# A diffusion backbone on one core: the first layer's FFNs in pairs by seven block products, and its row products moved

## The chip, the core and the metric

The kernel runs on one core of a Trainium2 chip. TensorE (PE) does the matmuls; VectorE (DVE), ScalarE (ACT) and GpSimd (POOL) do the elementwise work; SyncE (SP) issues the loads. The metric is the device time of one execution. The kernel before takes 2105.61 us, the median of three runs between 2104.49 and 2106.18 us.

## The reference

Two layers work on 256 latent and 256 context tokens of width 1024. Cut to what matters here:

```python
for l in range(DEPTH):
    mod = (silu_c @ w_ada[l] + b_ada[l])          # 9 x 1024 values: shift, scale, gate
    mod_c = (silu_cc @ w_ada[l] + b_ada[l])       # the same for the context
    x  = x  + 0.5 * g1  * swiglu(modulate(rmsnorm(x),  sh1,  sc1),  w1, w3, w2)   # d_ff 2816
    xc = xc + 0.5 * cg1 * swiglu(modulate(rmsnorm(xc), csh1, csc1), w1, w3, w2)
    o_lat, o_ctx = token_mixer(...)               # retention + latent attention, gated merge
    x  = x + g2 * o_lat
    x  = x + 0.5 * g3 * swiglu(...)               # the second FFN
    if not last:
        xc = xc + cg2 * o_ctx
        xc = xc + 0.5 * cg3 * swiglu(...)
return rmsnorm(x, final_norm)

def swiglu(h, w1, w3, w2):
    return (silu(h @ w1) * (h @ w3)) @ w2
```

The last layer's second FFN works on the latent tokens alone.

## The kernel before

Activations are kept transposed: eight tiles of 128 channels by 512 tokens, the latent ones in columns 0 to 255, the context's in 256 to 511. Every fp32 matmul is made of three single-pass ones: each operand is split into a high half (`hi`, rounded) and a low half (`lo` = operand - `hi`), and W.hi X.hi + W.lo X.hi + W.hi X.lo is accumulated (`mm3`). A weight tile is one chunk of 512 KB: SP loads it into one of four `raw` buffers, ACT writes its high half (`wh<-raw`), DVE its low half (`wl<-raw,wh`; four buffers of each). A chunk of kind `"d"` has the low half made without DVE: ACT writes the negative and a DMA from POOL's queue adds the operand (`wl<-raw`, `wl<-t`).

An FFN has 22 tiles of the inner width, worked off in parts. Each part does its up tiles (`up`: 24 matmuls of 512 columns for a tile of w1, 24 for a tile of w3, then silu, product and split into `G`), and then eight down tiles over the part's inner tiles (`down`), each of which updates x. `PARTS` are (0,6), (6,14), (14,22). In the first FFN's first part two more up tiles are computed early (`N_EARLY`). The last three down tiles of an FFN are worked in two halves of 256 columns (`tail`).

The first FFN of the second layer, (1, 2) in `PAIRED`, has the parts (0,4), (4,10), (10,16), (16,22). In its first part it works as above. After that it takes two inner tiles at a time: the weight tiles m and m+1 and the tokens (latent, context) form a 2x2 block product, which is done by seven half-size products in place of eight, by Winograd's form of Strassen's scheme. `blocks` builds the combined token operands t1 to t4 once, at the end of the first part. `split_pair` builds the combined weights of each pair: POOL makes s1 and s3, DVE s2 and s4, and each is then split into halves. `pair` issues the products: 84 matmuls of 256 columns, with four adds on DVE to combine them; two of its products are left for the next step (`pend`, `flush`).

The modulation values are dot products of rows of `w_ada` with silu(c). For all but the first two and the last of the 18 they are made by DVE: `ada_steps` loads eight chunks of 512 KB per value into `raw` buffers, and DVE multiplies each with the row of silu(c) and sums (`junk<-raw,crow`), in the first layer a second time for the context's row. They are called row products here. `ada_fill(n)` adds credit after a step and puts as many queued chunks there as the credit allows; `ada_flush` puts in all that must be done by then. `FILL` holds the credits.

All steps of the program go through `Plan`. It keeps an ordered list of all operations with a priority each (the place in the list; `ahead` moves one forward, row products are moved 200 back), gives each an assumed cost, and replays them engine by engine: whichever engine is free takes the waiting operation of the best priority whose inputs are ready and whose buffers (51 tiles `t`, 14 `u`, four `raw`, ...) can be had. This fixes each engine's order of instructions, which the hardware then keeps. `run_steps` issues loads and splits four chunks ahead of the step that uses them.

In the profile nearly all instructions carry line 378 of the kernel before, the line in `Plan.emit` that issues them (382 after the change); they are told apart by the names of their tiles.

Of the kernel before, what the change touches and what calls it, by code (L numbers as in the profile page):

```python
# [18 lines left out]
P = 128  # L19
KD = 8  # L20
# [431 lines left out]
def kernel(  # L452
# [152 lines left out]

    def split_pair(r0, r1):
# [14 lines left out]
        W["s4"] = halves(s4, hi[:, TOK:], lo[:, TOK:], S_DMA)  # L621
        W["a22"] = halves(a22, T(dt=F32R), T(dt=F32R))
        return W

    def run_steps():
        flat = [c for ch, _ in steps for c in ch]
        raws, ready = [], []

        def dma_to(n):
            for ap, size, _ in flat[len(raws):n]:  # L630
                raws.append(plan.new("raw", size))
                sp.dma_start(out=raws[-1], in_=ap)

        def split_to(n):
            dma_to(n)
            for i in range(len(ready), min(n, len(flat))):
                kind = flat[i][2]
                ready.append(split_pair(raws[i - 1], raws[i]) if kind == "p" else split_w(raws[i], flat[i][1], kind))
# [276 lines left out]
    def ffn(l, w1, w3, w2, m_sh, m_g, nrm_in, nrm_out, n_tok, n_next, fill, pre=None):  # L915
# [162 lines left out]
        for pi, (k0, k1) in enumerate(parts):  # L1078
# [4 lines left out]
            for m in range(at, until):  # L1083
                if pre and m < NS:
                    continue
                if paired and pi:
                    if (m - k0) % 2 == 0:
                        for j, w in enumerate((w1, w3)):
                            step(pair(j, m), chunk(w[l, m]), chunk(w[l, m + 1], kind="p"))
                elif m >= N_FIRST or pre:  # L1090
                    step(up(m), chunk(w1[l, m]), chunk(w3[l, m]))
# [13 lines left out]
            for m in range(KD - n_tail):  # L1105
                nrm = nrm_out if last else None
                step(down(m, k0, k1, nrm, 0, n_tok, m == KD - 1), chunk(w2[l, m, :, k0 * P:k1 * P], n))
                if m % 2 == 0 and not last:
                    ada_fill(FILL[0])
            if n_tail:  # L1110
# [16 lines left out]
    def mixer(l, nrm_in, nrm_out, full):  # L1127
# [461 lines left out]

        proj = [(rqk(RQ, i, NQ, 1.0), W("q", i)) for i in range(N_RQ[l], 4)]  # L1590
        proj += [(rqk(RK, i, TOK, RET_SCALE), W("k", i)) for i in range(4)]
        proj += [(rv(n, c), chunk(w_v[l, n, c])) for n in range(2) for c in range(4)]
        att = []
# [12 lines left out]
        for i, (f, w) in enumerate(proj):  # L1606
# [304 lines left out]
```

## Time and profile before

| what | value |
| --- | --- |
| median of three runs | 2105.61 us |
| the profiled execution | 2105.88 us |
| its span | 2104.1 us |
| PE busy | 2084.1 us (99%) |
| DVE busy | 1499.7 us (71%) |
| ACT busy | 839.4 us (40%) |
| POOL busy | 254.5 us (12%) |
| granted PE clock, mean | 0.996 |

The span runs from the first to the last instruction; the time of the execution is somewhat longer. An engine is busy while an instruction of it is under way; PE and the weight loads (PEld) overlap, and so do the ends of instructions that follow each other. A stretch of the span can be asked for by itself: the busy time of each engine in it, and the number of its instructions. The stretches below begin at the first matmul of a weight tile. In FFN1 of the first layer inner tiles 3 to 7 begin at 63.69 us, the first down tiles at 119.49, inner tiles 8 to 13 at 152.86. Merge (the gates, the MLA and retention outputs) is taken from the first MLA output tile at 681.81; its retention output tiles are 782.11 to 826.36. In FFN2 of the first layer the first down tiles begin at 940.24 and inner tiles 6 to 13 at 973.68. The second layer's paired FFN begins at 1241.86 us, its pairs at 1310.35, and its tail at 1579.37.

### The profile page before, as it was taken

What the parts mean: (1) busy time and instruction counts of PE and PEld (TensorE: products, weight loads), DVE (VectorE), ACT (ScalarE), POOL (GpSimd) and SP (SyncE); (2) the same over time, 40 slices, a digit from 0 to 9 for tenths busy, and PEclk for the clock granted to TensorE, in tenths of its full rate; (3) what the DMA queues carried; (4) which work ended last, traced back from release to release, by engine and by line L of the source; (5) the groups of instructions that cost most, each with busy time, mean ns of one, the idle gap of its engine ahead of it and who ended that gap; (6) DMA issues with size and microseconds to landing.
All of it is one profiled execution on the core that took longest, in us unless ns stands there. A gap on an engine that the chain in (4) does not pass through costs nothing.

```text
span 2104.1 us, 31948 instructions
## 1 busy us (share of the span) xinstructions
PE 2084.1 (99%) x12328; PEld 1816.7 (86%) x12328; DVE 1499.7 (71%) x2797; ACT 839.4 (40%) x1445; POOL 254.5 (12%) x268
## 2 busy tenths in 40 slices
PE   9999999999999999999999999999999999999998
PEld 7888888987788888988888898989999879999998
DVE  6898875678678435888865478877867867666655
ACT  5222122566443222422222243645456646344443
POOL 0000000211142000100000021332422114000000
PEclk9999999999999999999999999999999999999999
DMA  8476554221252333366655433654543326574653
GB/s 321 160 221 206 187 187 130 88 91 55 65 137 81 112 119 104 130 204 214 202 189 191 129 101 100 150 146 117 158 114 111 103 68 163 169 263 149 202 183 108
DMA packets 95722, 311.73 MB, mean 148 GB/s; under 512 B 10577, under 2 KB 13777, under 8 KB 95569
## 3 DMA queue, kind: packets, MB, share of 16 engines
q1 hardware_dynamic: 88082, 291.87, 42.9%
q0 software_dynamic: 7488, 17.83, 4.7%
q8 instruction: 97, 1.59, 0.3%
q14 instruction: 55, 0.45, 0.1%
HBM read 290.78 MB, written 1.05 MB: 139 GB/s over the span
## 4 chain that ended last, share of the span: by engine, by line
PE 90%; DVE 5%; DMA 2%; issue 1%; ACT 1%; POOL 1%; SPq 0%; POOLq 0%; DVEq 0%; ACTq 0%
PE m L378 82%; PE a L378 8%; DVE t L378 2%; DVE u L378 1%; DVE wl L378 1%; DMA wl<-t 1%; ACT wh L378 0%; DVE s L378 0%; DMA raw<-in_w3a_dram 0%; ACT t L378 0%; POOL t L378 0%; DMA x<-in_xT_dram 0%; POOL s L378 0%; DMA raw<-in_w1b_dram 0%; SPq L378 0%
## 5 line engine op out<-in xcount | busy, mean ns | idle before, releaser
L378 PE MATMUL m<-t,wh 128*128 128x512 f32 (+1 forms) x6236 | 1570.1, 340 | 2.4 <-DVE t L378 1.7
L378 PEld LDWEIGHTS m<-t,wh 128*128 128x128 f32 x6236 | 1073.6, 188 | 143.6 <-issue 1.9
L378 PE MATMUL m<-t,wl 128*128 128x512 f32 (+1 forms) x3118 | 1051.9, 339 | 0.6 <-DMA wl<-t 0.5
L378 ACT CAST wh<-raw 128x1024 fp32r<-128x1024 f32 (+2 forms) x388 | 391.8, 1011 | 753.7 <-PE m L378 609.0
L378 PEld LDWEIGHTS m<-t,wl 128*128 128x128 f32 x3118 | 587.0, 188 | 70.4 <-DMA wl<-t 1.2
L378 DVE TENSOR_TENSOR wl<-raw,wh 128x1024 fp32r<-128x1024 f32 (+2 forms) x372 | 437.3, 1177 | 177.3 <-ACT wh L378 175.4
L378 DVE SCALAR_TENSOR_TENSOR junk<-raw,crow 128x1024 f32<-128x1024 f32 x220 | 269.1, 1223 | 51.1 <-DMA raw<-in_w_ada_dram 48.5
L378 DVE SCALAR_TENSOR_TENSOR x<-m,mod,x 128x256 f32<-128x256 f32 x208 | 93.4, 479 | 102.4 <-PE m L378 101.9
L378 ACT ACTIVATE t<-m 128x512 f32<-128x512 f32 (+1 forms) x137 | 68.7, 503 | 243.3 <-PE m L378 240.0
L378 POOL TENSOR_TENSOR s<-s,mhalf 128x2 f32<-128x2 f32 (+1 forms) x31 | 32.5, 1053 | 1075.5 <-DVE s L378 1075.4
L378 DVE TENSOR_TENSOR t<-t,t 128x512 fp32r<-128x512 f32 (+7 forms) x234 | 137.7, 597 | 6.7 <-ACT t L378 4.0
L378 PE MATMUL m<-t,t 128*128 128x256 f32 (+1 forms) x696 | 102.3, 299 | 0.0
L378 PEld LDWEIGHTS m<-t,t 128*128 128x128 f32 x696 | 91.1, 190 | 4.0 <-issue 0.8
L378 PE MATMUL m<-wh,t 128*128 128x512 f32 x288 | 92.0, 399 | 0.0
L378 PE MATMUL a<-t,t 128*64 128x256 f32 (+3 forms) x512 | 87.6, 350 | 3.9 <-DVE t L378 3.8
L378 DVE TENSOR_TENSOR t<-t,m 128x512 f32<-128x512 f32 (+1 forms) x73 | 42.0, 577 | 64.3 <-PE m L378 63.2
L378 PEld LDWEIGHTS a<-t,t 128*128 128x128 f32 (+1 forms) x512 | 65.5, 175 | 20.2 <-DVE t L378 3.4
L378 DVE TENSOR_TENSOR u<-u,u 128x256 f32<-128x256 f32 x127 | 54.5, 447 | 14.4 <-ACT u L378 13.9
L378 PEld LDWEIGHTS m<-wh,t 128*128 128x128 f32 x288 | 53.1, 188 | 12.4 <-issue 1.2
L378 ACT CAST t<-t 128x512 fp32r<-128x512 f32 (+4 forms) x112 | 56.0, 527 | 12.2 <-DVE t L378 9.8
L378 PE MATMUL a<-t,wh 128*128 128x256 f32 x288 | 56.9, 281 | 0.0
L378 PE MATMUL m<-wl,t 128*128 128x512 f32 x144 | 56.7, 394 | 0.0
(127 smaller groups left out, 1574.8 us busy)
## 6 DMA issues: line engine op xcount, KB each, us to landing
raw<-in_w_ada_dram SPq DMA_DIRECT2D x122, 512.0 KB, 4.2
raw<-in_w_m_dram SPq DMA_DIRECT2D x76, 512.0 KB, 3.7
raw<-in_w1b_dram SPq DMA_DIRECT2D x44, 512.0 KB, 3.7
raw<-in_w3b_dram SPq DMA_DIRECT2D x44, 512.0 KB, 4.1
raw<-in_w1a_dram SPq DMA_DIRECT2D x41, 512.0 KB, 3.7
raw<-in_w3a_dram SPq DMA_DIRECT2D x41, 512.0 KB, 3.8
raw<-in_w2b_dram SPq DMA_DIRECT2D x32, 512.0 KB, 3.5
raw<-in_w2a_dram SPq DMA_DIRECT2D x32, 384.0 KB, 3.2
```

Source lines behind the costliest of these rows:

```text
L378: call(*[resolve(v) for v in args], **{k: resolve(v) for k, v in kwargs.items()})
```

## The change

FFN1 (0, 2) and FFN2 (0, 8) of the first layer get entries in `PAIRED`: FFN1 with the parts (0,6), (6,12), (12,18), (18,22), FFN2 with the parts of the second layer's. All parts but the first of each are worked in pairs. `S_DMA` becomes a table of which low halves of a pair are made by DMA: s4 alone, where s3 and s4 were; this holds for the second layer too. `FILL` becomes a table by layer and place. `BY_DMA` names the mixer's weights whose low half is made by DMA: `g` as before, and now each third of the first layer's `gr` and of the second layer's `gm`, and each second of the first layer's `v`.

```diff
-PAIRED = {(1, 2): ((0, 4), (4, 10), (10, 16), (16, 22))}
+PAIRED = {(1, 2): ((0, 4), (4, 10), (10, 16), (16, 22)), (0, 8): ((0, 4), (4, 10), (10, 16), (16, 22)),
+          (0, 2): ((0, 6), (6, 12), (12, 18), (18, 22))}
-S_DMA = True
+S_DMA = {2: ("s4",), 8: ("s4",)}
-FILL = (2,0,0,.5)
+FILL = {(0, 2): (.5, 1.5), (0, 8): (.5, 1), (1, 2): (.25, 1), (1, 8): (2, 2), 0: (.5, 0, 3), 1: (0, .75, .25)}
+BY_DMA = {("g", 0): 1, ("g", 1): 1, ("gr", 0): 3, ("gm", 1): 3, ("v", 0): 2}
...
-        W["s3"] = halves(s3, hi[:, 0:TOK], lo[:, 0:TOK], S_DMA)
+        W["s3"] = halves(s3, hi[:, 0:TOK], lo[:, 0:TOK], "s3" in by_dma)
...
+    def way(name, phase, i):
+        n = BY_DMA.get((name, phase), 0)
+        return "d" if n and i % n == 0 else "w"
...
-                            step(pair(j, m), chunk(w[l, m]), chunk(w[l, m + 1], kind="p"))
+                            step(pair(j, m), chunk(w[l, m], kind="d" if "a1" in S_DMA[m_g] else "w"), chunk(w[l, m + 1], kind=S_DMA[m_g]))
...
-                ada_fill(EARLY_FILL if pre and pi == 0 else FILL[0])
+                ada_fill(EARLY_FILL if pre and pi == 0 else FILL[l, m_g][0])
...
                 if m % 2 == 0 and not last:
-                    ada_fill(FILL[0])
+                    ada_fill(FILL[l, m_g][1])
...
-            ada_fill(FILL[1])
+            ada_fill(FILL[l][0])
...
-            step(g_step(i), W("g", i, "d"))
+            step(g_step(i), W("g", i, way("g", l, i)))
...
-            ada_fill(FILL[3])
+            ada_fill(FILL[l][2])
```

PE, first layer, FFN1: the first matmuls of inner tile 8. `wh`, `wl` are the halves of the tile of w1, the moving `t` are halves of the normalised tokens, `m` and `a` are PSUM tiles. Before:

```order
L378 MATMUL m2_1425<-t26_317,wh2_1336 128x512
L378 MATMUL m2_1425<-t26_317,wl2_1343 128x512
L378 MATMUL m2_1425<-t29_327,wh2_1336 128x512
L378 MATMUL m2_1425<-t39_375,wh2_1336 128x512
L378 MATMUL m2_1425<-t39_375,wl2_1343 128x512
L378 MATMUL m2_1425<-t42_386,wh2_1336 128x512
```

After, at the same place, rows eight to twelve of the first product and the start of the next:

```order
L382 MATMUL a0_1526<-t4_441,wl2_1433 128x256
L382 MATMUL a0_1526<-t2_458,wh2_1421 128x256
L382 MATMUL a0_1526<-t9_501,wh2_1421 128x256
L382 MATMUL a0_1526<-t9_501,wl2_1433 128x256
L382 MATMUL a0_1526<-t12_517,wh2_1421 128x256
L382 MATMUL m2_1547<-t0_857,wh3_1462 128x256
L382 MATMUL m2_1547<-t0_857,wl3_1479 128x256
L382 MATMUL m2_1547<-t49_867,wh3_1462 128x256
L382 MATMUL m2_1547<-t0_857,wh3_1462 128x256
L382 MATMUL m2_1547<-t0_857,wl3_1479 128x256
```

The wide accumulation over 512 tokens gives way to products of 256 columns; the one into `m2` has combined tokens (`t0`, `t49`) and combined weights (`wh3`).

SP, first layer, merge: loads between two MLA output tiles (`w_mo`); `w_m` are gate weights, `w_ada` row-product chunks, and the number after `raw` is the buffer. Before:

```order
L378 DMA raw0_6157<-in_w_mo_dram 128x1024
L378 DMA raw3_6206<-in_w_ada_dram 128x1024
L378 DMA raw3_6311<-in_w_m_dram 128x1024
L378 DMA raw2_6334<-in_w_m_dram 128x1024
L378 DMA raw1_6365<-in_w_mo_dram 128x1024
L378 DMA raw0_6408<-in_w_m_dram 128x1024
L378 DMA raw3_6451<-in_w_m_dram 128x1024
L378 DMA raw2_6487<-in_w_mo_dram 128x1024
L378 DMA raw1_6522<-in_w_ada_dram 128x1024
L378 DMA raw0_6552<-in_w_m_dram 128x1024
```

After:

```order
L382 DMA raw0_7040<-in_w_ada_dram 128x1024
L382 DMA raw2_7093<-in_w_ada_dram 128x1024
L382 DMA raw3_7242<-in_w_ada_dram 128x1024
L382 DMA raw1_7291<-in_w_m_dram 128x1024
L382 DMA raw1_7413<-in_w_m_dram 128x1024
L382 DMA raw0_7424<-in_w_mo_dram 128x1024
L382 DMA raw2_7460<-in_w_ada_dram 128x1024
L382 DMA raw1_7466<-in_w_ada_dram 128x1024
L382 DMA raw0_7507<-in_w_ada_dram 128x1024
L382 DMA raw3_7527<-in_w_m_dram 128x1024
```

Three chunks of row products stand in a row where one stood now and then, in three of the four buffers.

POOL, second layer, the first pair steps of the paired FFN: two adds that make s1 and s3, and the DMAs of low halves. Before:

```order
L378 TENSOR_TENSOR t42_11257<-raw3_11224 128x512
L378 TENSOR_TENSOR t46_11270<-raw2_11213,raw3_11224 128x512
L378 TENSOR_TENSOR t18_11312<-raw1_11277 128x512
L378 TENSOR_TENSOR t32_11329<-raw0_11245,raw1_11277 128x512
L378 DMA wl1_11338<-t46_11270 128x512
L378 DMA wl1_11338<-t44_11304 128x512
```

After:

```order
L382 TENSOR_TENSOR t49_13805<-raw2_13767 128x512
L382 TENSOR_TENSOR t17_13818<-raw0_13755,raw2_13767 128x512
L382 TENSOR_TENSOR t7_13838<-raw1_13798 128x512
L382 TENSOR_TENSOR t48_13855<-raw3_13779,raw1_13798 128x512
L382 DMA wl1_13887<-t27_13876 128x512
```

The DMA into the low half of s3 (the one from `t46`, written by the add before) is gone; that half is now a subtract in DVE's order.

## Rows read from the trace of the kernel before

**Rows 1.** The page: busy time of each engine, and the chain that ended last.
```profile
PE 2084.1 (99%) x12328; PEld 1816.7 (86%) x12328; DVE 1499.7 (71%) x2797; ACT 839.4 (40%) x1445; POOL 254.5 (12%) x268
...
PE 90%; DVE 5%; DMA 2%; issue 1%; ACT 1%; POOL 1%; SPq 0%; POOLq 0%; DVEq 0%; ACTq 0%
```

**Rows 2.** Busy times by stretch, first layer: two FFNs, then merge. Columns in the first line.
```profile
core 0: us, PE busy (x) PEld busy (x) DVE busy (x) ACT busy (x) POOL busy (x), PEclk, DMA share, GB/s
63.69:119.49 55.80, 55.80 (x241) 45.05 (x240) 48.33 (x81) 11.39 (x15) 0.00 (x0) 1.00 0.59 187
119.49:152.86 33.37, 33.37 (x146) 27.04 (x145) 31.27 (x54) 7.35 (x8) 0.00 (x0) 1.00 0.70 225
152.86:219.80 66.94, 66.94 (x289) 54.06 (x288) 56.19 (x93) 15.53 (x18) 0.00 (x0) 1.00 0.65 206
940.24:973.68 33.44, 33.44 (x145) 27.05 (x144) 30.85 (x55) 7.35 (x8) 0.00 (x0) 1.00 0.65 206
973.68:1062.65 88.97, 88.97 (x385) 72.07 (x384) 71.87 (x115) 20.74 (x24) 0.00 (x0) 1.00 0.65 205
681.81:782.11 100.30, 100.30 (x435) 81.18 (x434) 39.76 (x50) 26.30 (x34) 0.00 (x0) 1.00 0.35 114
782.11:826.36 44.25, 44.25 (x194) 36.04 (x192) 25.39 (x33) 13.25 (x16) 0.00 (x0) 1.00 0.33 109
```

**Rows 3.** The same by stretch: the FFN of the second layer that works in pairs.
```profile
1241.86:1310.35 68.49, 68.36 (x394) 59.74 (x393) 57.34 (x117) 28.12 (x58) 18.57 (x19) 1.00 0.25 78
1310.35:1404.33 93.98, 93.37 (x649) 86.83 (x648) 77.12 (x122) 46.83 (x87) 32.20 (x28) 1.00 0.56 147
1404.33:1497.93 93.60, 93.35 (x650) 86.80 (x648) 70.41 (x115) 46.33 (x86) 29.29 (x24) 1.00 0.52 135
1497.93:1592.98 95.05, 94.68 (x711) 90.30 (x710) 68.82 (x127) 51.14 (x100) 26.32 (x33) 1.00 0.52 136
1579.37:1592.98 13.61, 13.61 (x117) 13.61 (x116) 10.43 (x22) 7.22 (x14) 3.64 (x7) 1.00 0.48 163
1404.33:1461.70 57.37, 57.12 (x481) 56.91 (x480) 42.41 (x73) 34.03 (x67) 18.14 (x16) 1.00 0.58 137
```

**Rows 4.** Weight loads by group, 1404 to 1462 us: name, count | busy, mean ns.
```profile
L378 PEld LDWEIGHTS m<-t,wh 128*128 128x128 f32 x185 | 29.3, 189 | 0.0
```

**Rows 5.** DVE by form, 1404 to 1498 us: first and last of 11 groups, three between.
```profile
L378 DVE TENSOR_TENSOR u<-u,m 128x256 f32<-128x256 f32 x30 | 12.5, 416 | 8.8 <-PE m L378 6.2 <-ACT wl L378 2.4
...
L378 DVE TENSOR_TENSOR wl<-t,wh 128x512 fp32r<-128x512 f32 x12 | 11.3, 954 | 2.4 <-ACT wh L378 2.4
L378 DVE TENSOR_TENSOR wl<-raw,wh 128x768 fp32r<-128x768 f32 x8 | 7.6, 956 | 0.8 <-ACT wh L378 0.5
L378 DVE SCALAR_TENSOR_TENSOR x<-m,mod,x 128x256 f32<-128x256 f32 x16 | 7.0, 478 | 5.7 <-PE m L378 5.7
...
L378 DVE TENSOR_TENSOR u<-u,a 128x256 f32<-128x256 f32 x3 | 1.2, 416 | 0.0
```

**Rows 6.** The chain that ended last, 1404 to 1462 us: start, length, what.
```profile
1434.28 5.02 DMA wl<-t
```

**Rows 7.** DVE by form, whole span: row products, their reads, a small operation.
```profile
L378 DVE SCALAR_TENSOR_TENSOR junk<-raw,crow 128x1024 f32<-128x1024 f32 x220 | 269.1, 1223 | 51.1 <-DMA raw<-in_w_ada_dram 48.5
L378 DVE DVE_READ_ACCUMULATOR junk<-raw,crow 128x1 f32 x220 | 18.4, 83 | 0.0
L378 DVE TENSOR_TENSOR u<-u,u 128x256 f32<-128x256 f32 x127 | 54.5, 447 | 14.4 <-ACT u L378 13.9
```

**Rows 8.** Busy times of the first layer's attention stretch.
```profile
399.48:680.80 281.32, 279.45 (x1584) 235.48 (x1583) 211.29 (x536) 148.92 (x301) 69.71 (x67) 1.00 0.30 85
```

**Rows 9.** Instructions in order of time, DVE and POOL, 1409 to 1413 us.
```profile
1409.72 2.97 DVE L378 TENSOR_TENSOR wl<-t,wh 128x512 fp32r<-128x512 f32 x2 [1.86 <-ACT wh L378]
1409.15 1.29 POOL L378 TENSOR_TENSOR t<-raw 128x512 f32<-128x512 f32 x1 [5.26 <-DMA raw<-in_w3a_dram]
1410.41 1.73 POOL L378 TENSOR_TENSOR t<-raw,raw 128x512 f32<-128x512 f32 x1
```

**Rows 10.** Low halves made by DVE, tile wl: duration ns min/median/max.
```profile
L378 DVE TENSOR_TENSOR wl<-t,wh x36: 678/686/1776, 1306.5 to 1543.7; 128x512 fp32r<-128x512 f32 x36
```

More of the change, by code (lines that the diff above doesn't have):

```diff
@@ L604, in halves, with split_pair @@
         return Pair(hi, lo)
-    def split_pair(r0, r1):
+    def split_pair(r0, r1, by_dma):
         a11, a12, a21, a22 = r0[:, 0:TOK], r0[:, TOK:2 * TOK], r1[:, 0:TOK], r1[:, TOK:2 * TOK]
@@ L637, in split_to @@
                 kind = flat[i][2]
[L638 removed]
+                ready.append(split_pair(raws[i - 1], raws[i], kind) if isinstance(kind, tuple) else split_w(raws[i], flat[i][1], kind))
         at = 0
@@ L1088, in ffn @@
                         for j, w in enumerate((w1, w3)):
-                            step(pair(j, m), chunk(w[l, m]), chunk(w[l, m + 1], kind="p"))
+                            step(pair(j, m), chunk(w[l, m], kind="d" if "a1" in S_DMA[m_g] else "w"), chunk(w[l, m + 1], kind=S_DMA[m_g]))
                 elif m >= N_FIRST or pre:
-                    step(up(m), chunk(w1[l, m]), chunk(w3[l, m]))
+                    step(up(m), chunk(w1[l, m], kind=way("w1", (l, m_g), m)), chunk(w3[l, m], kind=way("w3", (l, m_g), m)))
                 elif m == 0:
                     step(first, *[chunk(w[l, i], kind="t" if i else "w") for i in range(N_FIRST) for w in (w1, w3)])
-                ada_fill(EARLY_FILL if pre and pi == 0 else FILL[0])
+                ada_fill(EARLY_FILL if pre and pi == 0 else FILL[l, m_g][0])
             at = until
@@ L1106, in ffn @@
                 nrm = nrm_out if last else None
-                step(down(m, k0, k1, nrm, 0, n_tok, m == KD - 1), chunk(w2[l, m, :, k0 * P:k1 * P], n))
+                step(down(m, k0, k1, nrm, 0, n_tok, m == KD - 1), chunk(w2[l, m, :, k0 * P:k1 * P], n, way("w2", (l, m_g), m)))
                 if m % 2 == 0 and not last:
-                    ada_fill(FILL[0])
+                    ada_fill(FILL[l, m_g][1])
             if n_tail:
@@ L1588, in mixer @@
             step(uq_step(c), chunk(w_uq[l, c], 768))
-        proj = [(rqk(RQ, i, NQ, 1.0), W("q", i)) for i in range(N_RQ[l], 4)]
-        proj += [(rqk(RK, i, TOK, RET_SCALE), W("k", i)) for i in range(4)]
-        proj += [(rv(n, c), chunk(w_v[l, n, c])) for n in range(2) for c in range(4)]
+        proj = [(rqk(RQ, i, NQ, 1.0), W("q", i, way("q", l, i))) for i in range(N_RQ[l], 4)]
+        proj += [(rqk(RK, i, TOK, RET_SCALE), W("k", i, way("k", l, i))) for i in range(4)]
+        proj += [(rv(n, c), chunk(w_v[l, n, c], kind=way("v", l, c))) for n in range(2) for c in range(4)]
         att = []
@@ L1624, in mixer @@
                     step(ret_split(i // 2 + 1))
-            ada_fill(FILL[2])
+            ada_fill(FILL[l][1])
         for i in range(4):
             for m in (2 * i, 2 * i + 1):
-                step(gate("gm", m), W("gm", m))
+                step(gate("gm", m), W("gm", m, way("gm", l, m)))
             if i == 0:
                 step(ret_out(3))
-            step(mo_step(i), chunk(w_mo[l, i]))
-            ada_fill(FILL[3])
+            step(mo_step(i), chunk(w_mo[l, i], kind=way("mo", l, i)))
+            ada_fill(FILL[l][2])
         for m in range(8):
-            step(gate("gr", m, m == 7), W("gr", m))
+            step(gate("gr", m, m == 7), W("gr", m, way("gr", l, m)))
             if m % 2:
-                ada_fill(FILL[3])
+                ada_fill(FILL[l][2])
         for m in range(8):
-            step(ro_step(m), chunk(w_ro[l, m]))
+            step(ro_step(m), chunk(w_ro[l, m], kind=way("ro", l, m)))
             if m % 2:
-                ada_fill(FILL[3])
+                ada_fill(FILL[l][2])
         ada_flush(l, SC3)
@@ L1645, in mixer @@
         for m in range(8 - n_tail):
-            step(o_step(m), chunk(w_o[l, m]))
+            step(o_step(m), chunk(w_o[l, m], kind=way("o", l, m)))
         if n_tail:
```

8 lines of the change are left out of this document (4 added, 4 removed).

## The prediction

> **What bounds the kernel now.** I read the page first. PE is busy 2084.1 of 2104.1 us and the chain that ended last is PE for 90% [rows 1]: a better order could win 20 us of idle PE at most, and a larger gain has to take matmul time away. Then I cut the span at the first matmuls of the weight tiles and read the busy times of each stretch. In the first layer's FFNs PE is busy to the last hundredth: 66.94 of 66.94 us, 33.37 of 33.37, 88.97 of 88.97, at a granted clock of 1.00, with DVE at 84%, 94% and 81% [rows 2]. So PE sets the time there, and DVE is next. The reader should also see that the kernel already holds what the change adds: the first FFN of the second layer works in pairs, in the three parts from 1310 to 1593 [rows 3].
>
> **What goes from PE.** An up step of a pair has 7 products x 4 k-tiles x 3 matmuls = 84 of 256 columns; it replaces two tiles of 24 matmuls of 512 columns. In the order of the changed program 14 such steps stand in FFN1 (its first part keeps 8 unpaired tiles, two of them computed early) and 18 in FFN2.
> - Unpaired: 12 tiles take 66.94 us in FFN1, 5.578 each; 16 take 88.97 in FFN2, 5.561 each [rows 2]. Two tiles are 11.156 and 11.121 us.
> - Paired: the three parts hold 18 pair steps, 21 down tiles and a tail of three. They take 93.98 + 93.60 + 95.05 = 282.63 us [rows 3]. Eight down tiles take 33.44 [rows 2], 21 take 87.78, the tail 13.61 [rows 3]. What is left, 181.24, is 10.07 us per pair step, PE's waits included.
> - The gain is 14 x 1.086 + 18 x 1.051 = 34.1 us. The last down parts get shorter (18 to 22, and 16 to 22, where 14 to 22 was), so 108 half-width matmuls of their tails become 54 wide ones: 0.4 us. Together 34.5.
>
> 84 matmuls in 10.07 us are 0.120 us each against 0.232 for 512 columns: half the columns at half the time, though each needs its own weights. The row shows that the load hides: 189 ns each, yet the 480 of six pair steps fit into 57.4 us [rows 4, 3]. The Trainium skill (TensorE: Matmul & The Clock Gate, Back-to-back issue gap) speaks against it: load and matmul together set the spacing, 131 ns sustained at 512 columns and 81 at 128. A line between these gives an estimate of 98 ns at 256; 84 x 98 against 48 x 131 would make a pair step 31% longer than what it replaces, some 111 us over 32 steps. The trace differs on both, 232 and 120 ns, and decides.
>
> The seven blocks are prepared at the end of part one by 48 DVE, 16 ACT and 8 POOL operations. In the second layer the stretch that holds them has PE busy 68.36 of 68.49 us [rows 3]; in the first layer they compete with row products, and I count them there.
>
> **What DVE gets.** Here the second layer is no copy: its two later parts carry no row products, and the first layer has two per chunk. I build a part's DVE time from the part 1404 to 1498. Its eleven groups sum to 75.7 us [rows 5] for 70.41 busy [rows 3], since ends overlap: a factor of 0.93. Eight down tiles (7.6 + 7.0) are 13.6 us with it; the other 56.8 are 9.47 per pair step. The change also takes one of two low halves made by DMA (s3) back to DVE: 0.954 x 0.93 = 0.89 [rows 5], so 10.36 us of DVE in a pair step of 10.07 us of PE, before any row product. For the second layer, with 5 or 6 single products in a part, that is 62.2 + 13.6 + 7.3 = 83 of 93.9 us, and no cost. Its chain now runs through 5.02 us of that DMA [rows 6]; the edit could give back the 1.2 us that PE waits in the three parts, or lose as much; I take 0.
>
> A chunk of row products is two multiplies of 1.223 and two reads of 0.083 us [rows 7], with the factor 2.43. In the changed order FFN1 has:
> - part one: 14 chunks where 16 were. 79.6 us busy in its two stretches [rows 2] + 48 operations of 0.4 us (0.447 less their overlap [rows 7]) - 4.9 = 93.9 against PE's 89.2: over by 4.7.
> - part two, 4 pair steps, 8 chunks: 41.4 + 13.6 + 19.4 = 74.4 against 73.7: over by 0.7.
> - part three, 6 pair steps, 9 chunks: 62.2 + 13.6 + 21.9 = 97.7 against 93.9: over by 3.8.
> - the last part has 2 chunks and some 12 us to spare.
>
> That is 9 us. From 119 to 153 operations overlap more (8 low halves, 16 updates of x and 16 products would sum to 36.2 us by their means and are busy 31.3); with 0.86 on all that is added 6 are left, which I take; bounds 0 and 9. FFN2 has 7 chunks in a full part: 62.2 + 13.6 + 17.0 = 92.8 against 93.9; I take 1 us for unevenness, bounds 0 and 3.
>
> **What moves to merge.** 36 chunks stand between the first merge weight and the output projection, where 6 were. Up to 782 us DVE has room: 39.76 busy of 100.30 [rows 2], and 19 more chunks less three low halves made by DMA give 82.6. Over the retention output it has none: 25.39 of 44.25 [rows 2] and 11 more chunks give 52.1, over by 7.9. These products are due much later (48 chunks finish the scale that the next FFN needs, and the 48th is the eighth of merge), so they may run on beside the output projection as far as four raw buffers let them: 1.5 us, bounds 0 and 8. Seven chunks stand among the attention steps, where PE idles 1.9 us now [rows 8]: 0.5, bounds 0 and 3.
>
> **Sum.** The profiled execution took 2105.88 us, 0.27 above the median of the runs and 1.8 above its span. 2105.9 - 34.5 + 6 + 1 + 1.5 + 0.5 = 2080.4, so 2080.
>
> **Rivals.**
> 1. *All of it is hidden*, since row products have the last priority and buffers even them out. For it: DVE at 94% without idle PE [rows 2]. Against it: 10.36 over 10.07. Then 2071.
> 2. *POOL and DVE block each other.* While POOL's two adds ran, from 1409.15 to 1412.14, two DVE subtracts took 2.97 us [rows 9] where the median one takes 0.686 [rows 10]. About 1.6 of the adds' 3.02 us are lost to DVE per pair step now, within the 9.47. A full DVE could lose the other 1.4 too: in the 10 steps of FFN1's middle parts and the 12 of FFN2's, with 2 us spare there, 29 us. Half of it gives 2094, all of it 2109. Against it: what DVE does on PSUM can run meanwhile. The Trainium skill (Advanced Engine Details and Errata, Miscellaneous Facts) says that the pool engine shares a read and a write interface with DVE and conflicts with operations of two SBUF inputs. The row agrees; a row product has two.
> 3. *Slower: row products clog the raw buffers in merge.* In the new order three of their chunks in a row take three of four raw buffers. Four groups of merge steps need 6 chunks in three tiles, 16.7 us, and eight need 5 in two, 11.1: a buffer may be held 11.1 and 8.9 us. Held 11.4 us, the 12 groups lose 4 x 0.4 + 8 x 3.1 = 26 us and all of the forecast's gain is gone; held 15 they lose 84, and the time is 2164. For it: DVE waits 48.5 us for such chunks now [rows 7], and 52.1 is over 44.25. Against it: 16 chunks passed in 33.4 us from 119 to 153, 8.3 us per buffer, and PE never waited [rows 2].
> 4. *The weight load binds.* At 189 ns one after the other [rows 4] a pair step takes 15.9 us and the kernel some 2265. The 10.07 us excludes it, unless the first layer differs.
>
> **Chances.** Forecast 0.48 (2074 to 2088), rival 1 0.24, rival 2 0.21, rival 3 0.06, rival 4 0.01. Between 2069 (rival 1 with the second layer's waits gone) and 2098 (rival 2 with two thirds of its price) lies some 0.84. A measurement can tell 0.2%, 4.2 us, from no change: only the end of rival 2 comes as near (0.03), and rivals 3 and 4 are slower. Faster 0.90, same 0.03, slower 0.07.
>
> **What would show it.** Right: net 2580 more matmuls of 256 columns and 1482 fewer of 512; pair steps of 84 at 0.120 us apart; 8 to 10 us more idle PE than now, most of it from 90 to 350 us, released by DVE's low halves or POOL's adds; DVE near 95% there. Wrong: a spacing over 0.13 us in the first layer's pairs, PE waiting in merge for a weight's DMA, or FFN2 losing as much as FFN1.

## The result and the profile after

Four runs of the changed kernel have a median of 2081.43 us (2080.36 to 2081.95), four of the kernel before, on the same chip, 2105.05 (2104.47 to 2106.18). The ratio is 0.9886, with a 95% interval of 0.9869 to 0.9904. The forecast was 2080 (2069 to 2098). The profiled execution took 2081.71 us, its span is 2079.9.

The total came out as worked out, but several terms of the sum didn't. The page first, which answers to [rows 1]:

```profile
PE 2052.6 (99%) x13426; PEld 1845.8 (89%) x13426; DVE 1714.4 (82%) x3301; ACT 967.0 (46%) x1773; POOL 388.9 (19%) x372
...
PE 79%; DVE 11%; issue 6%; ACT 2%; POOL 1%; DMA 1%; POOLq 0%; DVEq 0%; ACTq 0%; SPq 0%
```

PE is busy 31.5 us less and idle 27.3 us where it was 20.0. DVE is at 82% where it was at 71%. There are 1098 more matmuls, the net 2580 less 1482 that were expected.

Next the busy times by stretch of the changed kernel, cut as [rows 2, 3] at the first matmuls of the weight tiles. The columns are those of the first line.

```profile
core 0: us, PE busy (x) PEld busy (x) DVE busy (x) ACT busy (x) POOL busy (x), PEclk, DMA share, GB/s
0.00:69.33 69.33, 65.21 (x357) 50.73 (x357) 53.07 (x114) 32.00 (x68) 11.09 (x19) 0.93 0.74 270
69.33:125.13 55.80, 55.80 (x241) 45.05 (x240) 53.63 (x109) 16.95 (x30) 0.00 (x0) 1.00 0.42 140
125.13:158.53 33.40, 33.40 (x146) 27.03 (x145) 33.30 (x56) 9.40 (x13) 7.94 (x5) 1.00 0.65 217
158.53:231.96 73.43, 73.21 (x481) 66.72 (x479) 71.54 (x124) 31.47 (x56) 17.26 (x12) 1.00 0.54 163
232.19:326.74 94.55, 93.26 (x648) 86.51 (x647) 90.94 (x160) 43.49 (x80) 22.24 (x18) 1.00 0.55 165
158.53:391.89 233.36, 230.16 (x1605) 214.01 (x1604) 220.35 (x399) 111.09 (x209) 57.02 (x54) 1.00 0.54 159
391.89:417.13 25.24, 25.24 (x200) 25.24 (x201) 17.50 (x34) 14.86 (x36) 6.65 (x7) 0.93 0.29 94
463.37:536.64 73.27, 71.92 (x398) 55.95 (x397) 66.86 (x197) 44.43 (x112) 7.87 (x9) 1.00 0.35 108
678.20:778.35 100.15, 100.15 (x436) 81.14 (x435) 83.35 (x133) 29.57 (x37) 2.66 (x3) 1.00 0.75 233
778.35:822.83 44.48, 44.48 (x193) 36.03 (x192) 43.35 (x71) 13.02 (x16) 0.00 (x0) 1.00 0.66 210
868.64:893.66 25.02, 24.24 (x202) 23.84 (x201) 24.02 (x44) 12.56 (x26) 12.75 (x14) 1.00 0.22 76
893.66:1222.82 329.16, 326.29 (x2201) 299.90 (x2199) 302.71 (x549) 153.14 (x290) 73.65 (x55) 1.00 0.51 153
1291.37:1384.38 93.01, 93.01 (x649) 86.60 (x648) 85.07 (x141) 45.02 (x83) 28.30 (x21) 1.00 0.53 160
1726.66:1777.08 50.42, 48.31 (x411) 47.57 (x410) 47.44 (x131) 31.48 (x60) 23.54 (x28) 1.00 0.71 178
```

And those stretches of the kernel before that [rows 2, 3] don't hold: the start, the mixer's first steps, attention, FFN2's first step and its rest, the second layer's merge:

```profile
0.00:63.69 63.69, 61.56 (x356) 48.26 (x357) 47.19 (x111) 31.39 (x68) 2.56 (x11) 0.95 0.76 281
399.48:423.31 23.83, 23.83 (x202) 23.79 (x201) 15.36 (x27) 12.68 (x31) 8.50 (x12) 1.00 0.28 86
469.31:540.53 71.22, 70.82 (x398) 56.38 (x397) 57.44 (x175) 44.05 (x111) 8.74 (x7) 1.00 0.16 53
872.04:895.76 23.72, 23.72 (x203) 23.72 (x201) 22.91 (x48) 13.01 (x27) 7.04 (x6) 1.00 0.34 113
895.76:1241.86 346.10, 346.10 (x1571) 283.75 (x1570) 242.91 (x400) 84.82 (x111) 2.22 (x3) 1.00 0.57 182
1748.26:1801.20 52.94, 50.12 (x412) 49.37 (x410) 47.97 (x132) 29.50 (x58) 22.02 (x26) 0.97 0.57 141
```

From top to bottom:
- The start, to the first matmul of w1's tile 0: 69.33 us where it was 63.69. PE stands idle 4.1 us for 2.1, at a mean granted clock of 0.93 for 0.95. **+5.6**, forecast 0.
- Part one, up and down: 55.80 and 33.40, as before, with DVE at 53.63 and 33.30. PE waits for nothing.
- The paired parts of FFN1: 73.43 and 94.55 us. With all from the first pair to the mixer it is 233.36, and was 152.86 to 399.48 [rows 2, 8], 246.62. **-13.3**.
- The first steps of the mixer: 25.24, where it was 23.83, at clock 0.93. **+1.4**. Attention, from w_m's tile 8 to w_v: 73.27, and 71.22 before. **+2.1**. Both lie in the stretch for which 0.5 was forecast [rows 8]; with the small rest between them it is 4.0 longer.
- Merge and retention output: 100.15 and 44.48, where they were 100.30 and 44.25 [rows 2]. **0.1** in all, forecast 1.5. DVE's 83.35 in merge was forecast as 82.6.
- FFN2: its first step 25.02 for 23.72 (**+1.3**; POOL does 14 operations in it where it did 6), and the rest 329.16 for 346.10. **-16.9**.
- The second layer's paired FFN: the first of its three parts is 93.01 us where it was 93.98, and PE is never idle [rows 3]. The whole of it went from 282.63 to 280.06. **-2.6**, forecast 0.
- The last row lies in the second layer's merge, from w_m's tile 52 to w_mo's tile 4: 50.42 us, and 52.94 before. **-2.5**, forecast 0.

These come to -24.8; with the small rest the span is 24.2 us shorter. The pairs brought 30.2 us, where 27.5 was forecast (34.5 less 7 of waits in the two FFNs). What they brought beyond that, and the 5.1 us of the second layer, paid for the start, the mixer, attention and FFN2's first step.

The start needs a closer look. The busy times of the changed kernel there, with the granted clock:

```profile
core 0: us, PE busy (x) PEld busy (x) DVE busy (x) ACT busy (x) POOL busy (x), PEclk, DMA share, GB/s
54.00:60.58 6.58, 5.24 (x23) 3.69 (x22) 6.40 (x15) 2.52 (x4) 0.94 (x2) 1.00 0.00 0
60.58:62.70 2.12, 0.73 (x3) 0.30 (x3) 2.12 (x4) 0.00 (x0) 1.76 (x1) 0.84 0.00 0
62.70:69.33 6.63, 6.63 (x17) 5.18 (x17) 5.97 (x8) 1.79 (x3) 0.00 (x0) 0.54 0.87 278
```

PE waits 1.3 us for an ACT tile in the first row and 1.4 us for a DVE tile in the second, while DVE is busy 2.12 of 2.12 us. Then the granted clock is 0.50, which is 1.2 GHz of 2.4, for 6.83 us, most of the third row. (Another 6.83 us at 0.50 lie near 11 us in the kernel before, where the changed one has 3.41; so the two starts differ by less than what is lost at the end of this one.) Why DVE is late is seen in order of time (start, length, what), two rows of DVE in the changed kernel:

```profile
43.92 1.21 DVE L382 SCALAR_TENSOR_TENSOR junk<-wh,crow 128x1024 f32<-128x1024 f32 x1
45.07 1.83 DVE L382 SCALAR_TENSOR_TENSOR t<-u,mod,t 128x256 fp32r<-128x256 f32 x2
```

and POOL at that time and at the start's end:

```profile
44.62 1.11 POOL L382 TENSOR_TENSOR u<-t,t 128x256 f32<-128x256 f32 x1 [4.72 <-ACT t L382]
45.70 0.91 POOL L382 TENSOR_TENSOR u<-t 128x256 f32<-128x256 f32 x1
60.60 1.76 POOL L382 TENSOR_TENSOR u<-t,t 128x256 f32<-128x256 f32 x1 [5.66 <-ACT t L382]
```

The two DVE operations that begin at 45.07 take 1.83 us; such a pair takes 0.89 where nothing is beside it (a row of a run below). Beside them run two of POOL's subtractions, which belong to the seven blocks. There are eight. The prediction counted them in part one, where the code has them; POOL had nothing else queued and ran them as soon as each tile of the first norm was written, from 21.5 us on. Over the whole start the 16 operations `t<-u,mod,t` take 10.9 us in the changed kernel and 7.0 in the one before.

### The profile page after: what moved, and what is told of

It reads as the page before. It is cut to its first block, busy times and chain, and to the rows that moved or that the text cites. A ratio compares the mean times of both kernels' runs of the same rounds, so it can differ in the third digit from the quotient of the medians.

```text
span 2079.9 us, 35244 instructions
## 1 busy us (share of the span) xinstructions
PE 2052.6 (99%) x13426; PEld 1845.8 (89%) x13426; DVE 1714.4 (82%) x3301; ACT 967.0 (46%) x1773; POOL 388.9 (19%) x372
## 4 chain that ended last, share of the span: by engine, by line
PE 79%; DVE 11%; issue 6%; ACT 2%; POOL 1%; DMA 1%; POOLq 0%; DVEq 0%; ACTq 0%; SPq 0%
PE m L382 68%; PE a L382 11%; DVE t L382 5%; DVE u L382 2%; DVE wl L382 2%; DVE junk L382 1%; ACT t L382 1%; DVE s L382 1%; ACT wh L382 1%; POOL s L382 0%; POOL t L382 0%; DVE x L382 0%; DMA raw<-in_w1a_dram 0%; ACT wl L382 0%; DMA raw<-in_w2b_dram 0%
## 5 line engine op out<-in xcount | busy, mean ns | idle before, releaser
L382 PE MATMUL m<-t,wh 128*128 128x256 f32 (+1 forms) x6200 | 1442.2, 323 | 5.1 <-DVE u L382 2.3
L382 PE MATMUL m<-t,wl 128*128 128x256 f32 (+1 forms) x3100 | 990.6, 321 | 0.2 <-DVE wl L382 0.2
L382 PE MATMUL a<-t,wh 128*128 128x256 f32 x800 | 159.0, 282 | 1.4 <-ACT u L382 1.3
L382 ACT CAST wh<-t 128x512 fp32r<-128x512 f32 x200 | 116.8, 619 | 80.6 <-PE m L382 50.2
L382 PEld LDWEIGHTS a<-t,wh 128*128 128x128 f32 x800 | 129.9, 189 | 2.2 <-ACT u L382 1.8
L382 DVE TENSOR_TENSOR wl<-t,wh 128x512 fp32r<-128x512 f32 x150 | 121.9, 828 | 2.8 <-ACT wh L382 2.8
L382 DVE TENSOR_TENSOR u<-u,m 128x256 f32<-128x256 f32 x250 | 103.0, 414 | 24.4 <-PE m L382 22.4
L382 DVE TENSOR_TENSOR t<-t,t 128x256 fp32r<-128x256 f32 (+7 forms) x202 | 115.9, 584 | 5.3 <-ACT t L382 3.1
L382 PE MATMUL a<-t,wl 128*128 128x256 f32 x400 | 112.5, 281 | 0.3 <-DVE wl L382 0.3
L382 DVE TENSOR_TENSOR t<-raw,t 128x512 fp32r<-128x512 f32 (+1 forms) x120 | 103.0, 867 | 4.7 <-ACT t L382 4.6
```

The lines of the kernel that those rows point to most:

```text
L382: call(*[resolve(v) for v in args], **{k: resolve(v) for k, v in kwargs.items()})
```

## Experiments

Each edit is against the changed kernel. A stretch is always cut at the same matmuls. "Before" is the kernel before, run on the same chip beside the others, 2104.9 to 2105.8 us.

**FFN2 alone in pairs.** One entry less:

```diff
-PAIRED = {(1, 2): ((0, 4), (4, 10), (10, 16), (16, 22)), (0, 8): ((0, 4), (4, 10), (10, 16), (16, 22)),
-          (0, 2): ((0, 6), (6, 12), (12, 18), (18, 22))}
+PAIRED = {(1, 2): ((0, 4), (4, 10), (10, 16), (16, 22)), (0, 8): ((0, 4), (4, 10), (10, 16), (16, 22))}
```

> As the changed kernel, but the first layer's first FFN is unpaired as before; its credits of row products stay as changed. Theory A: the pairs of that FFN bring 13 to 15 us net of their own waits, and cost 5.6 us in the start and some 1.5 us after the shorter tail. Taking them out then gives 2081.4 + 13.3 - 5.6 - 1.4 = 2088. Rival: with row products beside them these pairs bring nothing, as DVE is full; then 2074 to 2081.

Measured: 2098.4 us, ratio 0.9969 (0.9958 to 0.998). Neither number was met. By stretch of this run, the start and then the rest of FFN1:

```profile
0.00:62.80 62.80, 61.41 (x356) 48.72 (x357) 47.05 (x110) 32.24 (x68) 2.54 (x11) 0.97 0.79 285
151.97:398.60 246.63, 246.63 (x1138) 202.66 (x1137) 128.26 (x200) 63.27 (x85) 6.62 (x13) 1.00 0.38 122
```

The start is 6.5 us shorter and POOL does 11 operations in it, as before the change, where the changed kernel has 19: the eight subtractions are gone, and with them the loss. The rest of FFN1 is 13.3 us longer, the mixer's first steps 1.4 shorter. Of the other 9 us 8.0 lie in the second layer's merge, with 3.41 us at half clock; this order leaves 28 multiplies of row products to the second layer, the changed kernel 20. So FFN1's pairs are worth 13.3 us where they stand, and give 6.5 back in the start.

**The subtractions after the start, on POOL.** The planner got a dependency on the last tile that the start writes, for the operations of the blocks (the same for all of them):

```diff
+    hold = []
...
                 e, f, g, h = U(), U(), U(), U()
+                if hold:
+                    plan.held.append(hold[0])
...
+                if hold:
+                    plan.held.pop()
...
-            gate_tile(pre["G"], banks.pop((m, 0)), banks.pop((m, 1)), m, 0, TOK)
+            hold[:] = [gate_tile(pre["G"], banks.pop((m, 0)), banks.pop((m, 1)), m, 0, TOK)]
```

> As the changed kernel, but POOL's eight subtracts for the first FFN's block operands wait until the third inner tile's gate is done. Theory A: the changed kernel's start is 5.6 us longer (69.3 against 63.7 us to the first matmul of a loaded tile) because these subtracts hold up DVE's operations on the same tokens, PE then waits twice 1.3 us and falls to half clock for 6.8 us. Then the start is 63.7 again and the time 2076, or up to 2 us more if the subtracts now disturb the first part. Rival: DVE is short of time in the start for other reasons (row products, order); then the start stays near 69 and the time near 2081.

Measured: 2080.9 us, ratio 0.9883 (0.9868 to 0.9897). It didn't test what it meant to. The dependency moved the operations in the written order, but on POOL no other work stood ahead of them; four rows of POOL in this run, then one of DVE, then the start:

```profile
44.99 1.05 POOL L382 TENSOR_TENSOR u<-t,t 128x256 f32<-128x256 f32 x1 [4.78 <-ACT t L382]
54.38 0.86 POOL L382 TENSOR_TENSOR u<-t,t 128x256 f32<-128x256 f32 x1 [7.06 <-DVE t L382]
55.19 1.71 POOL L382 TENSOR_TENSOR u<-t 128x256 f32<-128x256 f32 x1
61.00 1.10 POOL L382 TENSOR_TENSOR u<-t,t 128x256 f32<-128x256 f32 x1 [4.11 <-ACT t L382]
```

```profile
54.55 1.76 DVE L382 SCALAR_TENSOR_TENSOR junk<-wh,crow 128x1024 f32<-128x1024 f32 x1
```

```profile
0.00:66.61 66.61, 62.32 (x356) 48.53 (x357) 50.98 (x110) 31.36 (x68) 10.87 (x19) 0.97 0.73 269
```

They ran in the start as before, and PE waited 2.8 us for DVE there. The order that the planner wrote didn't bind, since POOL had nothing else to do first. The start took 66.61 us, without a half clock at its end; the 2.7 us that it was shorter than the changed kernel's were lost again in the rest of FFN1, 236.42 us for 233.36, with a wait of 2.4 and 3.41 us at half clock.

**The subtractions on DVE**, in all three FFNs that work in pairs. With the same dependency. There the order holds, since DVE has the start's work queued ahead of them:

```diff
-                pool.tensor_tensor(out=e, in0=b12.hi, in1=b11.hi, op=sub)
+                dve.tensor_tensor(out=e, in0=b12.hi, in1=b11.hi, op=sub)
...
-                pool.tensor_tensor(out=g, in0=b22.hi, in1=b12.hi, op=sub)
+                dve.tensor_tensor(out=g, in0=b22.hi, in1=b12.hi, op=sub)
```

> The changed kernel with the eight subtractions per FFN that feed the seven blocks' right-hand sides (e and g, 128x256) put on DVE in place of POOL, and in the first FFN not before the last tile of the start; the weight additions stay on POOL. Theory A (POOL's subtractions beside DVE's in the start stretch DVE there, TensorE waits some 2.7 us and then runs 6.83 us at clock 0.50): the start, 69.3 us to the first matmul of w1's tile 0, falls to 63.5 to 64.5, no half clock near 62 us, and the time is 2075 to 2077. Rival B (the start is long for another reason, the order of its tiles or the load of the pair's first tiles): the start stays at 69 us, and the eight subtractions of 0.35 us that now stand in part one, where DVE is at 96%, cost up to 3 us: 2081 to 2084.

Measured: 2073.55 us (2073.01 to 2074.89), ratio 0.9853 (0.9838 to 0.9868), better than either theory had it. The start and its end in this run:

```profile
0.00:62.62 62.62, 61.24 (x356) 48.45 (x357) 46.86 (x110) 31.89 (x68) 2.54 (x11) 0.97 0.78 284
50.00:56.00 6.00, 6.00 (x29) 5.00 (x28) 6.00 (x15) 2.75 (x4) 0.00 (x0) 1.00 0.00 0
56.00:62.62 6.62, 6.62 (x30) 5.45 (x30) 6.62 (x10) 2.64 (x6) 0.00 (x0) 1.00 0.46 133
```

and two rows of DVE, one in order of time (start, length), then the group of that form from 30 us to the start's end (count, busy us, mean ns):

```profile
57.87 0.89 DVE L382 SCALAR_TENSOR_TENSOR t<-u,mod,t 128x256 fp32r<-128x256 f32 x2
```

```profile
L382 DVE SCALAR_TENSOR_TENSOR t<-u,mod,t 128x256 fp32r<-128x256 f32 x10 | 4.4, 486 | 0.0
```

The start takes 62.62 us, 6.7 less; at its end PE is never idle and the clock stays at 1.00. The operation that was stretched takes 486 ns on the mean; in the changed kernel the same group has

```profile
L382 DVE SCALAR_TENSOR_TENSOR t<-u,mod,t 128x256 fp32r<-128x256 f32 x11 | 8.3, 781 | 0.2 <-ACT t L382 0.2
```

The extra subtractions on DVE in part one cost nothing: part one took 55.80 and 33.43 us. FFN2's first step, where eight more of them ran on POOL, took 24.48 us for 25.02. Theory A is shown: POOL's work beside DVE's made the loss in the start. The run before this one leaves no rival: on PE, DVE and ACT its instructions are the same in the same order up to the start's end, only POOL's eight subtractions are beside them, and its start takes 66.61 us for 62.62. That is 4.0 us without a half clock at the end.

**The weight additions on DVE.** The two POOL additions of `split_pair`:

```diff
-        pool.tensor_tensor(out=s1, in0=a21, in1=a22, op=ALU.add)
+        dve.tensor_tensor(out=s1, in0=a21, in1=a22, op=ALU.add)
...
-        pool.tensor_tensor(out=s3, in0=a11, in1=a21, op=ALU.subtract)
+        dve.tensor_tensor(out=s3, in0=a11, in1=a21, op=ALU.subtract)
```

> As the changed kernel, but the two adds that make s1 and s3 of each pair are on DVE in place of POOL. Theory A (POOL's adds and DVE's operations of two SBUF inputs block each other): two adds of 0.6 us come to DVE, and 1.6 us per pair step that DVE loses beside POOL's adds go; DVE has no more to do, two subtracts side by side take 1.3 us, not 3.0, and the time is 2079 to 2083. Rival (POOL's adds are free help): DVE gets 1.2 us more in each of 32 steps that are full already: 2095 to 2115.

Measured: 2073.28 us (2073.18 to 2073.5), ratio 0.9846 (0.9829 to 0.9862). It is under both numbers: FFN1's pairs are 2.2 us shorter, FFN2's 4.1, the second layer's the same to 0.01. FFN2 from the first matmul of its second step on, of this run:

```profile
889.76:1214.87 325.11, 325.11 (x2200) 299.92 (x2199) 294.46 (x585) 152.81 (x290) 16.23 (x19) 1.00 0.53 155
```

DVE does 36 operations more than in the changed kernel (585 for 549) and is busy 8.2 us less (294.46 for 302.71); PE is never idle. Counted over the whole trace of the changed kernel, 37 DVE subtractions `wl<-t,wh` of 512 columns had a POOL add or subtract beside them for over 0.3 us, and the median one took 1.43 us; the median of the 113 others is 0.68. Which one began first decides: 30 of the 37 began while POOL's was under way, median 1.45 us; the seven that began before POOL's took 0.68, as if alone. Then POOL's takes longer. The rows of the run with the held subtractions show both: DVE's row product at 54.55 us, begun beside POOL's of 54.38, takes 1.76 us (eight of them took 1.21 on the mean in the changed kernel's start), and POOL's at 55.19, begun beside that product, 1.71, where its like at 45.70 in the changed kernel took 0.91. An operation of DVE that reads PSUM isn't touched: `u<-u,m` takes 0.41 with POOL beside it (37) and without (213). So rival 2 of the prediction was partly true: the two engines block each other, for some 6 us in the two FFNs of the 29 that it allowed at most. (The time is 8 us less; this run's mixer also lacks 1.4 us, on which more below.)

**Both on DVE.** The edits of the last two together.

> The same, and also the two weight additions of each pair (s1 and s3) on DVE: POOL does no part of the pairs. If the two POOL costs are separate (8 us by the additions, about 5 by the subtractions in the start), the gains add: 2067 to 2069, start 63.5 to 64.5, the rest of the first FFN 231, of the second 325. If they are one cost seen twice, or DVE is now too full in part one: 2072 to 2075.

Measured: 2066.72 us (2066.56 to 2067.59), ratio 0.9819 (0.9803 to 0.9836). The gains add, as expected of two separate costs: 7.9 and 8.2 us apart, 14.7 together. This kernel is 38 us under the kernel before. The start is 63.95 us, with 6.83 us at half clock near 12 us, where the kernel with the subtractions alone on DVE has 3.41. The rest of FFN1 and of FFN2:

```profile
153.18:384.38 231.20, 229.52 (x1605) 213.80 (x1603) 215.83 (x425) 110.73 (x210) 19.84 (x30) 1.00 0.56 165
884.33:1208.68 324.35, 324.35 (x2201) 299.32 (x2199) 294.06 (x585) 151.92 (x288) 16.24 (x19) 1.00 0.53 156
```

FFN2 took 346.10 us before and takes 324.35 here, 21.75 less, and PE is busy all the time: that is what the pairs bring when nothing disturbs them. The same row was forecast with 18.9 and some tenths. In FFN1's row PE is idle 1.68 us, all of it one wait for an ACT tile just before the mixer. The row products stand here as in the changed kernel, so with POOL out of the pairs they cost these stretches nothing.

**A last part of six tiles**, with the changed kernel and with the one that has both on DVE:

```diff
-          (0, 2): ((0, 6), (6, 12), (12, 18), (18, 22))}
+          (0, 2): ((0, 6), (6, 10), (10, 16), (16, 22))}
```

> The changed kernel with only the parts of the first FFN changed to 6, 4, 6, 6 tiles: the same two answers without the rest. Theory A: the stretch to w_m tile 4 falls from 25.2 to 23.8 us or less, the half clock at 393 us goes, and the time is 2078 to 2080. Rival: 2081 to 2083.

> As the kernel without POOL in the pairs, and the parts of the first FFN 6, 4, 6, 6 hidden tiles wide in place of 6, 6, 6, 4, so that the last part is 6 wide. Theory A (the mixer's start loses 1.4 us, with 3.41 us at half clock, because a last part of 4 tiles is too short to cover the norm between): the stretch to the mixer's w_m tile 4 falls from 25.2 to 23.8 or less with no half clock at 393 us, and the time is 1.4 to 3 us under that kernel's. Rival (the norm's chain of DVE and ACT steps starts with the last down tiles whatever the part): no difference, within 1 us, or 1 us slower since the second part now has 4 tiles.

Measured: 2079.83 us (2079.05 to 2084.39), ratio 0.9886 (0.9871 to 0.9901), and 2067.15 (2065.8 to 2068.5), ratio 0.9821 (0.9807 to 0.9836). Neither time tells the theories apart: the first is 1.6 us under the changed kernel's, within the spread of its own four executions; the second is 0.4 over that of both on DVE, as the rival has it. The mixer's first steps took 23.8 and 23.7 us, as theory A says, and PE doesn't wait before them. But they took 23.7 or 23.8 also in five runs with the short part: in the two kernels with the additions on DVE, in the first one with the subtractions held on POOL, and in the next two below, whose first layer is that of the changed kernel to the instruction. In all of these PE waits 1.7 us for an ACT tile there, as in the changed kernel, and the clock stays at 1.00; of the seven traces with this wait the clock fell in two, the changed kernel's and that with the subtractions on DVE. So the wait alone doesn't decide whether the clock falls, and theory A isn't shown; what decides is open. The 1.4 us come and go between executions.

**s3's low half back to DMA in the second layer.**

```diff
-S_DMA = {2: ("s4",), 8: ("s4",)}
+S_DMA = {(0, 2): ("s4",), (0, 8): ("s4",), (1, 2): ("s3", "s4")}
...
-                            step(pair(j, m), chunk(w[l, m], kind="d" if "a1" in S_DMA[m_g] else "w"), chunk(w[l, m + 1], kind=S_DMA[m_g]))
+                            step(pair(j, m), chunk(w[l, m], kind="d" if "a1" in S_DMA[l, m_g] else "w"), chunk(w[l, m + 1], kind=S_DMA[l, m_g]))
```

> The changed kernel with one entry put back: in the second layer's paired FFN the low half of s3 is again made by DMA beside that of s4, as in the kernel before; the first layer's pairs keep s4 alone. Theory A (the 2.57 us that this stretch lost between the two kernels, 282.63 to 280.06 us, come from s3's return to DVE, which I had costed at nothing): the stretch is back at 282 to 283 us and the time 2083 to 2085. Rival B (they come from the fewer row products in that stretch): the stretch stays at 280.0 to 280.3 and the time at 2081 to 2082.

Measured: 2088.47 us, ratio 0.9921 (0.9904 to 0.9937). The stretch takes 285.87 us, 5.8 more than the changed kernel and 3.2 more than before. What PE waited for in it (us in total, times, longest):

```profile
PE a L382 <- DVE wl L382: 2.0, 1, 2.0
PE m L382 <- DMA wl<-t: 1.9, 3, 1.3
```

and the DMA issues of these low halves (count, KB, median us from issue to landing):

```profile
wl<-t POOLq DMA_DIRECT2D x34, 256.0 KB, 5.2
```

A landing takes 5.2 us, where the kernel before has 3.8 with 36 of them and the changed one 3.7 with 17. Rival B is out, and theory A holds with a larger sum than it gave: s3's return is worth 5.8 us beside the new places of the row products, not 2.6. The new order puts 20 multiplies of row products into the second layer, which had none before; that they, and the DMAs that bring their weights, make this route 3.2 us dearer than before is likely, but wasn't tried by itself.

**gm's low halves on DVE in the second layer.**

```diff
-BY_DMA = {("g", 0): 1, ("g", 1): 1, ("gr", 0): 3, ("gm", 1): 3, ("v", 0): 2}
+BY_DMA = {("g", 0): 1, ("g", 1): 1, ("gr", 0): 3, ("v", 0): 2}
```

> The changed kernel without the entry that makes every third low half of the second layer's gm weights by DMA: they are all made on DVE, as before the change. Theory A (this entry is what took 2.52 us from the stretch between w_m tile 52 and w_mo tile 4 of the second layer, 52.94 to 50.42 us, where the kernel before fell to clock 0.50): the stretch is back at 52.5 to 53.5 us with a half clock in it, and the time is 2083 to 2085. Rival B (the row products that left that stretch are the cause): 50.4 to 50.6 us, no half clock, 2081 to 2082.

Measured: 2082.38 us (2079.86 to 2084.16), ratio 0.989 (0.9875 to 0.9904). The stretch of this run:

```profile
1725.41:1778.58 53.17, 49.99 (x412) 49.25 (x410) 49.55 (x132) 29.38 (x58) 21.85 (x26) 0.97 0.58 151
```

53.17 us at clock 0.97, with 3.41 us at 0.50, where the changed kernel has 50.42 at 1.00: what theory A says of the stretch, in one profile of each. The total doesn't show it: 2082.38 and 2081.43 us have ratios whose intervals overlap. In the two profiles the mixer's 1.4 us and 0.5 us of the start stand against it.

**The row products back in their old places.**

```diff
-FILL = {(0, 2): (.5, 1.5), (0, 8): (.5, 1), (1, 2): (.25, 1), (1, 8): (2, 2), 0: (.5, 0, 3), 1: (0, .75, .25)}
+FILL = {(0, 2): (2, 2), (0, 8): (2, 2), (1, 2): (2, 2), (1, 8): (2, 2), 0: (0, 0, .5), 1: (0, 0, .5)}
```

> As the changed kernel, but row products stand where they stood before the change (two chunks per inner tile, eight per down part, half a chunk per two merge tiles). Theory A: DVE bounds as soon as its work exceeds PE's. A part of six inner tiles gets 20 chunks: about 59 us for its pair steps, 13 for its down tiles and 46 for row products are 118 us of DVE against 94 of PE, 25 us over; 16 over in the part of four, 8 in the last, 45 in the second FFN. That is 2081 + 90 = 2170, clearly slower than before. Rival: row products have the last priority and are hidden wherever they stand: 2075 to 2085.

Measured: 2198.3 us, ratio 1.0437 (1.0417 to 1.0457). The rest of FFN1 and of FFN2 in this run:

```profile
155.29:450.24 294.95, 252.15 (x1606) 224.74 (x1604) 282.88 (x513) 114.54 (x214) 63.66 (x57) 0.96 0.59 175
950.38:1338.92 388.54, 347.49 (x2200) 310.38 (x2198) 351.04 (x631) 155.41 (x291) 77.91 (x55) 0.96 0.55 169
```

and PE's two largest waits in the first of them:

```profile
PE m L382 <- DVE u L382: 13.7, 7, 3.0
PE m L382 <- DVE wl L382: 10.1, 13, 3.1
```

Theory A, with a larger loss than its 2170. Each row is some 60 us longer, where it had 49 and 45. In the first DVE is busy 282.88 of 294.95 us and PE idle 42.8, and 23.9 us pass at clock 0.50, where half the time is lost, 12 us; in the second these are 30.7 and 15. With the row products in their old places the pairs make this kernel 4% slower; that the row products move out is what makes them pay.

## Why the prediction was right, and where it wasn't

- *What goes from PE.* Right in kind and somewhat low. Part two of FFN1 took 73.43 us; less eight down tiles, 33.40, four pair steps have 10.01 each, where 10.07 was taken and 73.7 us forecast. Undisturbed, FFN2 gives 21.75 us, not 19.
- *The weight load* hides: 84 matmuls in 10.01 us are 0.119 us each, though a load takes 189 ns [rows 4]. Rival 4 is out.
- *DVE in part one*, 93.9 against 89.2: too high. It was busy 86.93, and PE never waited. *In part three*, 97.7 against 93.9: 90.94, with PE idle 1.3 us. The groups of part three sum to 102.5 us for 90.94 busy, so ends overlap by a factor of 0.887 and not 0.93. A factor from a part where DVE is busy 75% was too high for one at 96%, and DVE at 96 to 100% didn't stall PE. So the 7 us that the forecast took for DVE's overload aren't seen: without POOL in the pairs the same row products cost nothing, which is what rival 1 said. It isn't so wherever they stand, as the old places show.
- *The place of the loss.* This is the step that failed: "in the first layer they compete with row products, and I count them there". The blocks' POOL operations have inputs that are ready in the start and no work ahead of them, so they ran there, beside a DVE that is busy 6.40 of 6.58 us near the start's end and feeds PE. The 6 us were taken for parts one and three; the start lost 5.6. That the two numbers are close is luck.
- *The signs.* The spacing came as written, and the count of matmuls. PE's idle time grew by 7.3 us, near the 8 to 10, but not by the waits that were named: in the rest of FFN1 PE waits 3.0 us for ACT and 0.2 for a low half by DVE. And a sign of being wrong came true, "FFN2 losing as much as FFN1": against the kernel with both on DVE the rest of FFN2 loses 4.8 us and that of FFN1 2.2, where 1 and 6 were forecast.
- *s3's return to DVE* was put at 0, and *gm by DMA* wasn't priced: the first gave 2.6 us or more, the second 2.5 where it saves a half clock. The first could be read: the chain ran through 5.02 us of that DMA [rows 6], and the part's PE was idle 0.6, 0.25 and 0.4 us [rows 3]. The prediction said the sign was open and kept to the idle time that it saw, 1.2 us. It got those and 1.4 of PE's own busy time, 281.40 to 280.06, which no idle time showed.
- *Merge*: right. DVE 83.35 for 82.6, nothing lost, and rival 3 is out: 36 chunks passed, and PE was idle 0 us in 144.6.
- *Attention*: +4.0 for 0.5 in the stretch of [rows 8], over its bounds of 0 to 3. Of this 1.4 is the mixer's half clock; 2.1 lie from w_m's tile 8 to w_v, and for these no run was made.
- *Rival 2* (POOL and DVE block each other) had 0.21 as an alternative to the forecast. It is no alternative: it is at work in the forecast's own case, for 6 us in the pairs and 6.7 in the start, 2.7 of these as waits and about 3.4 by the half clock. Here the Trainium skill (Advanced Engine Details and Errata, Miscellaneous Facts), by which the pool engine conflicts with DVE operations of two SBUF inputs, agrees with the 0.68 and 1.43 us. It agrees with the row products too, which read two as well, once it is asked which began first: of the 11 that had POOL beside them nine began before POOL's operation and took 1.22 us, as alone; the two that began after it took 1.71.

So the total was right partly because errors cancelled: 2.7 us more from the pairs and 5.1 us not seen in the second layer, against 8.4 us not seen in the start, the mixer's first steps and FFN2's first step.

## What to carry to other kernels

An operation given to an idle engine didn't wait here for the place where the code has it: it started when its inputs were ready, so cost it there, beside what is busy at that time. Moving small SBUF work from a full DVE to an idle POOL can make DVE slower (the changed kernel's DVE is busy 1714.4 us, the one that has both on DVE 1692.5); count DVE's busy time with and without it before taking POOL for free. And when a neighbouring DMA route is relieved, look for the gain in the whole stretch, not only in the waits that the profile names.

## What the runs showed of the hardware that was not expected

- Six of the kernels have the same instructions in the same order up to the end of the start, and PE waits 1.3 and 1.4 us there in each. In two of the traces 6.83 us at half clock follow (the changed kernel's, and that with the additions on DVE), in three 3.41 us, and in one, that with the row products in their old places, none: the start takes 66.09 us there for 69.33. A short wait of PE can cost more than its length, and the same wait doesn't always.
- Most DVE operations of one form doubled beside POOL (`wl<-t,wh`, 0.68 to 1.43 us) while most of another kept their time (row products, 1.22 us), though both read two SBUF tiles. The order of their beginnings tells them apart: 30 of 37 began after POOL's operation, but 2 of 11 row products. In both forms the one that began second took longer (1.45 and 1.71 us) and the one that began first didn't.
